# A transformer layer on one core: one more summed pair in the last gate/up block, squares written to PSUM, and another order of pairs in the second down block

## The chip, the cores and the metric

The kernel runs on one core of one Trainium2 chip. The metric is the device time of one execution in microseconds (us). A core has five engines with a queue of instructions each: TensorE (PE in the profile, with its weight loads as PEld), VectorE (DVE), ScalarE (ACT), GpSimd (POOL) and SyncE (SP), which issues most DMA transfers. Each engine executes its queue in order and waits on semaphores where an instruction needs another engine's result. All data are fp32.

## The reference, cut to what matters

The layer works on 256 positions of 2048 values. The change touches its last part, the gated feed-forward layer and the final norm:

```python
h = h + jnp.einsum('bse,ed->bsd', y, w_out[l])
u = rmsnorm(h, ln2_w[l])
ff = jax.nn.silu(jnp.einsum('bsd,df->bsf', u, w_ffn_gate[l])) * jnp.einsum('bsd,df->bsf', u, w_ffn_up[l])
h = h + jnp.einsum('bsf,fd->bsd', ff, w_ffn_down[l])
return rmsnorm(h, final_norm_w)      # h * rsqrt(mean(h * h) + eps) * final_norm_w
```

with `d` = 2048 and `f` = 5632. The projections ahead of it, a recurrence and a retention, are not touched.

## The kernel before, in words

**One product.** TensorE multiplies in a format that keeps fewer digits, so each operand is split in two: ScalarE casts it to a high part (`wh`, `ah`, `sh`, `bh`; L123) and VectorE subtracts that from the operand for the low part (`wl`, `al`, `sl`, `bl`; L124). A product of a 128x128 left with a 128x512 right is three matmuls: high times low, low times high, high times high (`three`, L683 to L685).

**Pairs.** The inner dimension is taken in pairs of 128 rows: 8 pairs for a gate/up block, 22 for a down block. With the two halves of the positions and two column blocks of 512, each pair is a 2x2 by 2x2 block product, added up in four PSUM tiles c11, c12, c21 and c22. A plain pair takes eight products (`EIGHT`). A summed pair takes seven after Winograd's form of Strassen's scheme (`SEVEN`): its operands are sums, on the left of activations (`Left`; names s, sh, sl), on the right of weights (`add`, L661, four additions on VectorE that overwrite the raw tile).

**Blocks.** Blocks 0 and 1 are the output projection, 2 to 12 the eleven gate/up blocks, 13 and 14 the two down blocks of 1024 columns each. `SUMMED` names the summed pairs of each block, `STEPS` the order of its steps: p is a plain pair and h half of one; s is the four products of a summed pair of the *next* block that all its pairs share (`share`); d is the three products that are left of a summed pair of this block (`direct`). After the last s the four shared sums are combined once (L806 to L813): p1 is a copy of c11, p = c12 - p1, q = p - c22, q goes back to c12's bank by ScalarE (L811), and c22 and c21 are corrected from q and p. The first down block has three of its summed pairs so prepared (`EARLY_DOWN`); the others of the down blocks (`SUMMED_DOWN`) are done whole, into banks p1, p5, p6 and p7, which VectorE adds to the rows `htok` once the last of them is through (`post` in `down_block`: n, part and htok rows, L923 to L934). `ORDER_DOWN` gives the order of the 22 pairs in each down block.

**Left sides.** `make_left(i)` splits the activations of pair i for the down blocks and, where the pair is summed, builds their sums. It runs when the pair's first weights are loaded.

**End of a block.** In the first down block each c is added to `htok` (L945), and `down_post` squares the row on ScalarE with a running sum (L983; the squares themselves go to an act tile `junk` that nobody reads), then multiplies the row by the norm weight `fw` (L988, deferred). The second down block ends with two plain pairs as four tails, one c after another, each cut into narrow splits.

**What sets the order.** The code is one list of steps, with weights loaded three halves ahead. The framework's scheduler then orders the instructions of each engine by a model of the chip and by priorities, which follow the order of the code; semaphores and pools do the rest. `act_tile` takes one of 60 tiles of 128x512, `raw_tile` one of 7 of 128x1024, `split_tiles` a wh and a wl out of 4, and PSUM has eight banks in two pools of four (`bank`, `aux`), chosen by the parity of the block (`room`). A tile is handed out again when the last reader of its old contents is through; whoever writes it first waits for that.

Of the kernel before, what the change touches and what calls it, by code (L numbers as in the profile page):

```python
# [28 lines left out]

SUMMED = ((), (4, 5), (2, 3), (1, 2, 3)) + ((0, 1, 2, 3),) * 8 + ((1, 2, 3),)
SUMMED_OUT, SUMMED_FFN = (4, 5), (0, 1, 2, 3)

PLAIN = ((4, 5, 6, 7, 0, 1, 2, 3),) * 2 + (tuple(range(8)),) * 11
STEPS = ("pppspppspp", "ppspdpsdpp", "pdpsdpspspp", "pspsdpsdpsdp") + ("psdhsdhsdhsdhp",) * 7 + ("psdpsdpsddp", "psdpsdpsdpp")


EARLY_DOWN = (0, 1, 2)
SUMMED_DOWN = (9, 12, 15, 17, 19), (5, 7, 9, 11, 12, 13, 15, 17, 19)  # L40
ORDER_DOWN = (3, 4, 0, 5, 6, 1, 7, 8, 2) + tuple(range(9, 22)), (0, 12, 1, 19, 2, 5, 3, 7, 4, 9, 6, 11, 8, 13, 10, 15, 14, 17, 16, 18, 20, 21)
BESIDE = (12, 19)


# [1 line left out]
def tile_hymba_layer(ctx: ExitStack, tc: tile.TileContext, A: dict, out: bass.AP):  # L46
# [22 lines left out]
    def act_tile(name, dt=F32):  # L69
        return apool.tile([P, 512], dt, tag="act", name=nm(name))  # L70
# [717 lines left out]
    class Block:  # L788
# [8 lines left out]
        def share(self, m):  # L797
            left, right, last = self.lefts[self.summed[m]], self.shared[m].parts, m == len(self.summed) - 1
            ps = self.ps
            for c, a, b in (("c11", "a11", "b11"), ("c22", "s1", "t1"), ("c21", "s3", "t3"), ("c12", "s2", "t2")):  # L800
                if m == 0:
                    ps[c] = room(self.index)(c)
                three(ps[c], left[a], right[b], m == 0, last)
            if not last:
                return

            p1, p, q = (act_tile(x) for x in ("p1", "p", "q"))
            act.copy(out=p1, in_=ps["c11"])
            v.tensor_tensor(out=p, in0=ps["c12"], in1=p1, op=ALU.subtract)
            v.tensor_tensor(out=q, in0=p, in1=ps["c22"], op=ALU.subtract)  # L810
            act.copy(out=ps["c12"], in_=q)  # L811
            v.tensor_tensor(out=ps["c22"], in0=q, in1=ps["c21"], op=ALU.subtract)
            v.tensor_tensor(out=ps["c21"], in0=ps["c21"], in1=p, op=ALU.subtract)  # L813

        def direct(self, m, quad):
            for c, a, b in DIRECT:
# [17 lines left out]
        def put(self, after):  # L834
            plain = [i for i in PLAIN[self.index] if i not in self.summed]
            for k, kind in enumerate(self.steps):
                if kind == "p":
                    i, n = plain.pop(0), len(plain)
                    quad = Quad(self.src(i), False)
                    quad.brief = n == 0  # L840
                    run = lambda i=i, quad=quad, k=k, n=n: self.plain(i, quad, k == 0, n == 0)
                elif kind == "h":
                    at = self.steps[:k].count("h") % 2
                    if not at:
                        i = plain.pop(0)
                        whole = Quad(self.src(i), False)
                    quad = HalfOf(whole, at)
                    some = slice(4 * at, 4 * at + 4)
                    run = lambda i=i, quad=whole, some=some: self.plain(i, quad, False, False, some)
                elif kind == "d":  # L850
                    m = self.steps[:k].count("d")
                    quad = Direct(self.shared[m])
                    run = lambda m=m, quad=quad: self.direct(m, quad)
                else:
                    m = self.steps[:k].count("s")
                    quad = after.shared[m]
                    run = lambda m=m: after.share(m)
                program.append(([quad], run))

    def ffn_post(j):  # L860
# [50 lines left out]
    def down_block(d, ahead):  # L911
        ps = {} if d else ahead.ps

        def tile_of(c):
            return 2 * d + int(c[2]) - 1, int(c[1]) - 1

        def into(c, a, b=None, op=ALU.add):

            h = htok[tile_of(c)]
            t = a  # L920
            if b is not None:
                t = act_tile("part")
                v.tensor_tensor(out=t, in0=a, in1=b, op=ALU.subtract)  # L923
            v.tensor_tensor(out=h, in0=h, in1=t, op=op)
            return t

        def post(c):
            if c == "p1":
                ps["a1"] = act_tile("part")
                act.copy(out=ps["a1"], in_=ps[c])  # L930
                into("c11", ps["a1"])
            elif c == "p7":
                n = act_tile("n")
                v.tensor_tensor(out=n, in0=ps["p6"], in1=ps["a1"], op=ALU.subtract)  # L934
                into("c12", n, ps["p5"])
                m = into("c21", n, ps["p7"], ALU.subtract)
                into("c22", m, ps["p5"])
            elif c[0] == "c":
                cb, t = tile_of(c)
                if d and c[:3] == "c22":  # L940
                    c0 = S * (c == "c22b")
                    down_post(cb, t, c0, S, ps[c][:, c0 : c0 + S])
                else:
                    h = htok[cb, t]
                    v.tensor_tensor(out=h, in0=ps[c], in1=h, op=ALU.add)  # L945
                    down_post(cb, t, 0, 512)

        n = FT // 2
        quads = []
        for i in ORDER_DOWN[d]:  # L950
            if d == 0 and i in EARLY_DOWN:
                quads.append(Direct(ahead.shared[EARLY_DOWN.index(i)]))
            else:
                quads.append(Quad(A["w_down"][d * n + i], i in SUMMED_DOWN[d], lambda i=i: make_left(i)))
            quads[-1].pair = i
        if d:
            quads[-1].apart = quads[-2].apart = True
        tail = [("c11", 0, 512), ("c12", 0, 512), ("c21", 0, 512)]
        def half_over():
            h = htok[3, 1][:, S:]  # L960
            act.copy(out=h, in_=ps["c22"][:, S:])
            v.tensor_tensor(out=ps["c22b"][:, S:], in0=ps["c22b"][:, S:], in1=h, op=ALU.add)

        early = {}
        if d:

            early["c22"] = lambda: v.tensor_tensor(out=ps["c22"], in0=ps["c22"], in1=htok[3, 1], op=ALU.add)
            early["c22b"] = half_over
            tail[:0] = [("c22b", S, S, slice(0, 1))]
            tail += [("c22", 0, S), ("c22b", S, S, slice(1, 4))]  # L970
        else:
            tail.append(("c22", 0, 512))

        block(NB + 2 + d, quads, dl, post, ps, tail, early=early, ordered=d == 1)

    def down_post(cb, t, c0, cw, src=None):

        h = htok[(cb, t)][:, c0 : c0 + cw]
        src = h if src is None else src
        f = fw[cb][:, c0 : c0 + cw]  # L980
        n = cb + (c0 > 0)
        j = act_tile("junk")
        act.activation(out=j[:, :cw], in_=src, func=AF.Square, accum_out=ssq[:, t, n : n + 1])  # L983
        p = pre[:, t : t + 1]
        if cb < 3:
# [278 lines left out]
```

## Time and profile before

| | before |
|---|---|
| time, median of 3 runs | 1084.82 us (1084.63 to 1085.21) |
| profiled execution | 1085.53 us |
| its span | 1083.7 us |
| granted clock of TensorE, mean | 0.996 |
| TensorE busy | 1072.3 us, 99% |
| VectorE busy | 972.0 us, 90% |
| ScalarE busy | 666.9 us, 62% |
| GpSimd busy | 56.5 us, 5% |
| DMA | 244.62 MB, 226 GB/s |

The span is the time between the first and the last instruction that the profile shows; 1.83 us of the execution lie around it. The granted clock is the share of its full speed, 2.4 GHz, that the chip gave to TensorE; 0.50 is 1.2 GHz. In a timeline a row gives the start and the duration of an instruction, or of several in a row (x3), and in brackets how long the engine had been idle before it and what ended that. Records of neighbouring matmuls overlap: the distance of their starts is what one costs.

### The profile page before, as it was taken

What the parts mean: (1) busy time and instruction counts of PE and PEld (TensorE: products, weight loads), DVE (VectorE), ACT (ScalarE), POOL (GpSimd) and SP (SyncE); (2) the same over time, 40 slices, a digit from 0 to 9 for tenths busy, and PEclk for the clock granted to TensorE, in tenths of its full rate; (3) what the DMA queues carried; (4) which work ended last, traced back from release to release, by engine and by line L of the source; (5) the groups of instructions that cost most, each with busy time, mean ns of one, the idle gap of its engine ahead of it and who ended that gap; (6) DMA issues with size and microseconds to landing.
All of it is one profiled execution on the core that took longest, in us unless ns stands there. A gap on an engine that the chain in (4) does not pass through costs nothing.

```text
span 1083.7 us, 14591 instructions
## 1 busy us (share of the span) xinstructions
PE 1072.3 (99%) x5083; PEld 897.5 (83%) x5083; DVE 972.0 (90%) x1411; ACT 666.9 (62%) x951; POOL 56.5 (5%) x73
## 2 busy tenths in 40 slices
PE   9999999999999999999999999999999999999997
PEld 7888888888888888888888888888888888878886
DVE  7789889988878889989999999999999899999886
ACT  7756744468746676656656566565656666655463
POOL 0603230000000000000000000000000010000001
PEclk9999999999999999999999999999999999999998
DMA  9964574554557587677776777776777856557662
GB/s 328 351 211 154 176 252 168 181 176 165 185 194 236 188 306 277 227 242 247 257 269 229 250 262 238 265 269 227 251 249 228 273 170 219 194 174 240 208 214 78
DMA packets 71386, 244.62 MB, mean 226 GB/s; under 512 B 8208, under 2 KB 8592, under 8 KB 71312
## 3 DMA queue, kind: packets, MB, share of 16 engines
q1 hardware_dynamic: 68400, 236.34, 64.3%
q0 software_dynamic: 1472, 4.72, 1.3%
q10 hardware_dynamic: 1440, 2.62, 0.6%
q8 instruction: 40, 0.66, 0.2%
q14 instruction: 34, 0.28, 0.1%
HBM read 239.46 MB, written 4.19 MB: 225 GB/s over the span
## 4 chain that ended last, share of the span: by engine, by line
PE 94%; POOL 1%; DMA 1%; DVE 1%; issue 1%; ACT 1%; SPq 0%; POOLq 0%; ACTq 0%
PE c L683 22%; PE c L685 22%; PE c L684 22%; PE fm L194 10%; PE fm L196 5%; PE tm L174 2%; PE tm L176 2%; PE tm L175 2%; PE p L685 1%; PE p L684 1%; PE p L683 1%; POOL sumsq L310 1%; PE ft L868 1%; DMA raw<-in_w_lx 1%; DMA raw<-in_w_v 0%
## 5 line engine op out<-in xcount | busy, mean ns | idle before, releaser
L123 ACT CAST wh<-raw 128x1024 fp32r<-128x1024 f32 (+1 forms) x500 | 464.5, 960 | 321.6 <-PE c L685 127.3
L124 DVE TENSOR_TENSOR wl<-raw,wh 128x1024 fp32r<-128x1024 f32 (+1 forms) x500 | 543.1, 1114 | 73.0 <-ACT wh L123 71.2
L684 PE MATMUL c<-wl,ah 128*128 128x512 f32 x814 | 317.7, 390 | 0.0
L685 PE MATMUL c<-wh,al 128*128 128x512 f32 x814 | 314.9, 389 | 0.0
L683 PE MATMUL c<-wh,ah 128*128 128x512 f32 x814 | 276.8, 392 | 0.0
L683 PEld LDWEIGHTS c<-wh,ah 128*128 128x128 f32 x814 | 153.4, 188 | 31.8 <-ACT wh L123 0.3
L685 PEld LDWEIGHTS c<-wh,al 128*128 128x128 f32 x814 | 152.8, 188 | 31.7 <-DVE al L124 0.3
L684 PEld LDWEIGHTS c<-wl,ah 128*128 128x128 f32 x814 | 152.9, 188 | 31.3
L194 PE MATMUL fm<-u,wh 128*128 128x512 f32 x512 | 161.3, 396 | 0.0
L196 PEld LDWEIGHTS fm<-u,wl 128*128 128x128 f32 x512 | 96.0, 188 | 22.5
L196 PE MATMUL fm<-u,wl 128*128 128x256 f32 x512 | 100.9, 278 | 0.0
L661 DVE TENSOR_TENSOR raw<-raw,raw 128x512 f32<-128x512 f32 x118 | 81.1, 688 | 2.0
L661 DVE TENSOR_TENSOR raw<-raw 128x512 f32<-128x512 f32 x118 | 80.6, 686 | 1.1
L194 PEld LDWEIGHTS fm<-u,wh 128*128 128x128 f32 x512 | 78.3, 189 | 0.3
L684 PE MATMUL c<-wl,sh 128*128 128x512 f32 x194 | 75.2, 389 | 0.0
L685 PE MATMUL c<-wh,sl 128*128 128x512 f32 x194 | 74.0, 389 | 0.0
L683 PE MATMUL c<-wh,sh 128*128 128x512 f32 x194 | 68.7, 391 | 0.3 <-ACT sh L123 0.3
L175 PE MATMUL tm<-wl,u 128*128 128x512 f32 x128 | 48.8, 394 | 0.0
L176 PE MATMUL tm<-wh,u 128*128 128x512 f32 x128 | 48.5, 390 | 0.0
L174 PE MATMUL tm<-wh,u 128*128 128x512 f32 x128 | 47.1, 398 | 0.8 <-ACT u L298 0.8
L1119 POOL DMA_DIRECT2D htok<-kept_rows x8 | 4.3, 546 | 796.4 <-DVE wl L124 704.0
L683 PEld LDWEIGHTS c<-wh,sh 128*128 128x128 f32 x194 | 36.4, 188 | 8.2 <-ACT sh L123 0.7
(247 smaller groups left out, 1076.2 us busy)
## 6 DMA issues: line engine op xcount, KB each, us to landing
raw<-in_w_gu SPq DMA_DIRECT2D x216, 512.0 KB, 5.1
raw<-in_w_down SPq DMA_DIRECT2D x91, 512.0 KB, 4.8
raw<-in_w_out SPq DMA_DIRECT2D x34, 512.0 KB, 4.3
raw<-in_w_lx SPq DMA_DIRECT2D x16, 512.0 KB, 6.9
raw<-in_w_k SPq DMA_DIRECT2D x16, 512.0 KB, 3.5
raw<-in_w_q SPq DMA_DIRECT2D x16, 512.0 KB, 3.7
raw<-in_w_rg SPq DMA_DIRECT2D x16, 512.0 KB, 3.5
raw<-in_w_lg SPq DMA_DIRECT2D x16, 512.0 KB, 3.4
```

Of the source, the lines that this page charges most:

```text
L123: act.copy(out=dst_h, in_=src)
L124: v.tensor_tensor(out=dst_l, in0=src, in1=dst_h.bitcast(F32), op=ALU.subtract)
L174: pe.matmul(ps, ah, wh, start=first, stop=False)
L175: pe.matmul(ps, ah, wl, start=False, stop=False)
L176: pe.matmul(ps, al, wh, start=False, stop=last)
L194: pe.matmul(ps, wh, hl, start=n + i == 0, stop=False)
L196: pe.matmul(ps[:, :S], wl, hl[:, :S], start=False, stop=n + i == len(order) - 1)
L310: pool.tensor_tensor(out=sumsq, in0=sumsq, in1=sq, op=ALU.add)
L661: v.tensor_tensor(out=dst, in0=a, in1=b, op=ALU.add)
L683: pe.matmul(p, ah, bh, start=first, stop=False, skip_group_check=onto)
L684: pe.matmul(p, ah, bl, start=False, stop=False, skip_group_check=onto)
L685: pe.matmul(p, al, bh, start=False, stop=last, skip_group_check=onto)
```

## The change

Block 12, the last gate/up block, gets four summed pairs like the others, and the steps of blocks 11 and 12 follow: block 11 is now "psdhsdhsdhsdhp" and block 12 "psdpsdpsddp". The six instructions that combine the shared sums are given a higher priority (offset 300) in all blocks. `ASIDE` lets block 12 make the lefts of down pairs 1 to 4 ahead of its steps 0, 2, 4 and 6. In the second down block the first two pairs are plain ones, and the pairs behind them are ordered anew; near the end, summed pair 17 stands ahead of 16, 18, 20 and 21 before, and behind 16 now. In the first down block the squares of the norm are written over the PSUM bank of the c that has just been added, in place of an act tile; in the second they stay as they are. Line numbers move by one to four: L123 is now L124, L811 is L813, L983 is L987, L988 is L992.

```diff
--- before.py
+++ after.py
@@ -29,16 +29,17 @@
 
 
 
-SUMMED = ((), (4, 5), (2, 3), (1, 2, 3)) + ((0, 1, 2, 3),) * 8 + ((1, 2, 3),)
+SUMMED = ((), (4, 5), (2, 3), (1, 2, 3)) + ((0, 1, 2, 3),) * 9
 SUMMED_OUT, SUMMED_FFN = (4, 5), (0, 1, 2, 3)
 
 PLAIN = ((4, 5, 6, 7, 0, 1, 2, 3),) * 2 + (tuple(range(8)),) * 11
-STEPS = ("pppspppspp", "ppspdpsdpp", "pdpsdpspspp", "pspsdpsdpsdp") + ("psdhsdhsdhsdhp",) * 7 + ("psdpsdpsddp", "psdpsdpsdpp")
+STEPS = ("pppspppspp", "ppspdpsdpp", "pdpsdpspspp", "pspsdpsdpsdp") + ("psdhsdhsdhsdhp",) * 8 + ("psdpsdpsddp",)
 
 
 EARLY_DOWN = (0, 1, 2)
+ASIDE = {(12, 0): 1, (12, 2): 2, (12, 4): 3, (12, 6): 4}
 SUMMED_DOWN = (9, 12, 15, 17, 19), (5, 7, 9, 11, 12, 13, 15, 17, 19)
-ORDER_DOWN = (3, 4, 0, 5, 6, 1, 7, 8, 2) + tuple(range(9, 22)), (0, 12, 1, 19, 2, 5, 3, 7, 4, 9, 6, 11, 8, 13, 10, 15, 14, 17, 16, 18, 20, 21)
+ORDER_DOWN = (3, 4, 0, 5, 6, 1, 7, 8, 2) + tuple(range(9, 22)), (0, 1, 12, 2, 19, 3, 5, 4, 7, 6, 9, 8, 11, 10, 13, 14, 15, 16, 17, 18, 20, 21)
 BESIDE = (12, 19)
 
 
@@ -805,12 +806,13 @@
                 return
 
             p1, p, q = (act_tile(x) for x in ("p1", "p", "q"))
-            act.copy(out=p1, in_=ps["c11"])
-            v.tensor_tensor(out=p, in0=ps["c12"], in1=p1, op=ALU.subtract)
-            v.tensor_tensor(out=q, in0=p, in1=ps["c22"], op=ALU.subtract)
-            act.copy(out=ps["c12"], in_=q)
-            v.tensor_tensor(out=ps["c22"], in0=q, in1=ps["c21"], op=ALU.subtract)
-            v.tensor_tensor(out=ps["c21"], in0=ps["c21"], in1=p, op=ALU.subtract)
+            with tc.high_priority(offset=300):
+                act.copy(out=p1, in_=ps["c11"])
+                v.tensor_tensor(out=p, in0=ps["c12"], in1=p1, op=ALU.subtract)
+                v.tensor_tensor(out=q, in0=p, in1=ps["c22"], op=ALU.subtract)
+                act.copy(out=ps["c12"], in_=q)
+                v.tensor_tensor(out=ps["c22"], in0=q, in1=ps["c21"], op=ALU.subtract)
+                v.tensor_tensor(out=ps["c21"], in0=ps["c21"], in1=p, op=ALU.subtract)
 
         def direct(self, m, quad):
             for c, a, b in DIRECT:
@@ -855,6 +857,8 @@
                     m = self.steps[:k].count("s")
                     quad = after.shared[m]
                     run = lambda m=m: after.share(m)
+                if (self.index, k) in ASIDE:
+                    program.append(([], lambda i=ASIDE[self.index, k]: make_left(i)))
                 program.append(([quad], run))
 
     def ffn_post(j):
@@ -943,7 +947,7 @@
                 else:
                     h = htok[cb, t]
                     v.tensor_tensor(out=h, in0=ps[c], in1=h, op=ALU.add)
-                    down_post(cb, t, 0, 512)
+                    down_post(cb, t, 0, 512, gone=None if d else ps[c])
 
         n = FT // 2
         quads = []
@@ -973,13 +977,13 @@
 
         block(NB + 2 + d, quads, dl, post, ps, tail, early=early, ordered=d == 1)
 
-    def down_post(cb, t, c0, cw, src=None):
+    def down_post(cb, t, c0, cw, src=None, gone=None):
 
         h = htok[(cb, t)][:, c0 : c0 + cw]
         src = h if src is None else src
         f = fw[cb][:, c0 : c0 + cw]
         n = cb + (c0 > 0)
-        j = act_tile("junk")
+        j = act_tile("junk") if gone is None else gone
         act.activation(out=j[:, :cw], in_=src, func=AF.Square, accum_out=ssq[:, t, n : n + 1])
         p = pre[:, t : t + 1]
         if cb < 3:
```

Up to some 775 us of the run all engines have the same rows in the same order. Over the whole run TensorE has 3 matmuls fewer, VectorE 7 rows more (four raw additions and three splits), ScalarE 3 more and SP one load more. Three places are shown. The names in the rows are tiles, with a running number that differs between the two kernels.

ScalarE at the start of the second down block, before: casts of weights (`wh`, `bh`) and the four squares of the first down block (L983), in the order of the queue.

```order
L123 CAST wh_1951_9147<-raw_1950_9145 128x1024
L123 CAST wh_1954_9153<-raw_1953_9151 128x1024
L123 CAST wh_1957_9159<-raw_1956_9157 128x1024
L123 CAST bh_1960_9165<-raw_1959_9163 128x512
L123 CAST wh_1967_9231<-raw_1966_9229 128x1024
L983 ACTIVATE junk_1962_9182,ssq_120<-htok_1826_8628 128x512
L123 CAST wh_1969_9239<-raw_1959_9163 128x1024
L983 ACTIVATE junk_1963_9197,ssq_120<-htok_1828_8632 128x512
L983 ACTIVATE junk_1964_9212,ssq_120<-htok_1827_8630 128x512
L983 ACTIVATE junk_1965_9227,ssq_120<-htok_1829_8634 128x512
L123 CAST bh_1984_9289<-raw_1983_9287 128x512
L123 CAST wh_1971_9243<-raw_1966_9229 128x1024
```

And now (the squares are L987):

```order
L124 CAST wh_1962_9172<-raw_1961_9170 128x1024
L124 CAST wh_1965_9178<-raw_1964_9176 128x1024
L124 CAST bh_1971_9246<-raw_1970_9244 128x512
L124 CAST wh_1968_9240<-raw_1967_9238 128x1024
L987 ACTIVATE c11_1678_7960,ssq_120<-htok_1831_8641 128x512
L987 ACTIVATE c12_1681_7972,ssq_120<-htok_1833_8645 128x512
L987 ACTIVATE c21_1680_7968,ssq_120<-htok_1832_8643 128x512
L124 CAST wh_1978_9280<-raw_1977_9278 128x1024
L124 CAST bh_1991_9334<-raw_1990_9332 128x512
L987 ACTIVATE c22_1679_7964,ssq_120<-htok_1834_8647 128x512
L124 CAST wh_1980_9288<-raw_1970_9244 128x1024
L124 CAST wh_1982_9292<-raw_1977_9278 128x1024
```

Each square now writes to the bank of the c that it belongs to; three stand together ahead of the casts of the first summed pair, and the fourth behind two of these.

VectorE at the end of block 12, before: p, q and the two corrections (L809 to L813), among splits of weights (`wl`, wide) and of lefts (`al`, narrow).

```order
L124 TENSOR_TENSOR wl_1726_8162<-raw_1722_8155,wh_1725_8161 128x1024
L809 TENSOR_TENSOR p_1714_8126<-c12_1668_7925,p1_1713_8125 128x512
L810 TENSOR_TENSOR q_1715_8127<-p_1714_8126,c22_1666_7917 128x512
L124 TENSOR_TENSOR wl_1734_8202<-raw_1730_8195,wh_1733_8201 128x1024
L812 TENSOR_TENSOR c22_1666_7917<-q_1715_8127,c21_1667_7921 128x512
L813 TENSOR_TENSOR c21_1667_7921<-c21_1667_7921,p_1714_8126 128x512
L124 TENSOR_TENSOR wl_1739_8238<-raw_1737_8235,wh_1738_8237 128x1024
L124 TENSOR_TENSOR al_1724_8158<-ff_1013_4924,ah_1723_8157 128x512
L124 TENSOR_TENSOR wl_1742_8244<-raw_1740_8241,wh_1741_8243 128x1024
L124 TENSOR_TENSOR al_1732_8198<-ff_1092_5290,ah_1731_8197 128x512
```

And now (p is L811, q L812, the corrections L814 and L815; L883 is the gating of block 12's own outcome):

```order
L125 TENSOR_TENSOR t4l_1715_8110<-raw_1711_8097,t4h_1714_8109 128x512
L811 TENSOR_TENSOR p_1726_8168<-c12_1681_7972,p1_1725_8167 128x512
L125 TENSOR_TENSOR wl_1739_8215<-raw_1737_8212,wh_1738_8214 128x1024
L125 TENSOR_TENSOR wl_1747_8257<-raw_1745_8254,wh_1746_8256 128x1024
L812 TENSOR_TENSOR q_1727_8169<-p_1726_8168,c22_1679_7964 128x512
L125 TENSOR_TENSOR wl_1744_8251<-raw_1742_8248,wh_1743_8250 128x1024
L883 SCALAR_TENSOR_TENSOR gated_1740_8224<-c12_1590_7573,r2_tok_110,gated_1740_8224 128x512
L883 SCALAR_TENSOR_TENSOR gated_1741_8232<-c22_1588_7565,r2_tok_110,gated_1741_8232 128x512
L125 TENSOR_TENSOR wl_1759_8314<-raw_1752_8298,wh_1758_8313 128x1024
L814 TENSOR_TENSOR c22_1679_7964<-q_1727_8169,c21_1680_7968 128x512
L815 TENSOR_TENSOR c21_1680_7968<-c21_1680_7968,p_1726_8168 128x512
```

Two wide splits stand between p and q now, and the corrections of c22 and c21 behind the gating.

VectorE near the end of the second down block, before: the last summed pair's additions to the rows (n is L934, part L923, htok L924) and the narrow splits (`bl`) of the last two pairs. The difference n, two parts and two wide splits stand ahead of these rows.

```order
L924 TENSOR_TENSOR htok_2040_9569<-htok_2040_9569,part_2124_9984 128x512
L924 TENSOR_TENSOR htok_2039_9567<-htok_2039_9567,part_2125_9987 128x512
L923 TENSOR_TENSOR part_2126_9990<-part_2125_9987,p5_1987_9303 128x512
L124 TENSOR_TENSOR bl_2132_10005<-raw_2130_10002,bh_2131_10004 128x512
L124 TENSOR_TENSOR bl_2134_10009<-raw_2130_10002,bh_2133_10008 128x512
L124 TENSOR_TENSOR bl_2137_10039<-raw_2135_10036,bh_2136_10038 128x512
L124 TENSOR_TENSOR bl_2139_10043<-raw_2135_10036,bh_2138_10042 128x512
L924 TENSOR_TENSOR htok_2041_9571<-htok_2041_9571,part_2126_9990 128x512
L124 TENSOR_TENSOR bl_2142_10049<-raw_2140_10046,bh_2141_10048 128x512
L124 TENSOR_TENSOR bl_2144_10053<-raw_2140_10046,bh_2143_10052 128x512
L124 TENSOR_TENSOR bl_2147_10084<-raw_2145_10081,bh_2146_10083 128x512
L124 TENSOR_TENSOR bl_2149_10088<-raw_2145_10081,bh_2148_10087 128x512
```

And now (n is L938, part L927, htok L928, L971 an addition of htok to c22's bank); n and one part stand right ahead:

```order
L927 TENSOR_TENSOR part_2134_10036<-n_2132_10031,p7_1996_9356 128x512
L928 TENSOR_TENSOR htok_2041_9581<-htok_2041_9581,part_2133_10033 128x512
L928 TENSOR_TENSOR htok_2040_9579<-htok_2040_9579,part_2134_10036 128x512
L927 TENSOR_TENSOR part_2135_10039<-part_2134_10036,p5_1994_9348 128x512
L125 TENSOR_TENSOR bl_2138_10048<-raw_2136_10045,bh_2137_10047 128x512
L125 TENSOR_TENSOR bl_2140_10052<-raw_2136_10045,bh_2139_10051 128x512
L928 TENSOR_TENSOR htok_2042_9583<-htok_2042_9583,part_2135_10039 128x512
L125 TENSOR_TENSOR bl_2143_10058<-raw_2141_10055,bh_2142_10057 128x512
L125 TENSOR_TENSOR bl_2145_10062<-raw_2141_10055,bh_2144_10061 128x512
L125 TENSOR_TENSOR bl_2148_10093<-raw_2146_10090,bh_2147_10092 128x512
L971 TENSOR_TENSOR c22_1975_9258<-c22_1975_9258,htok_2042_9583 128x512
L125 TENSOR_TENSOR bl_2150_10097<-raw_2146_10090,bh_2149_10096 128x512
```

No wide split stands between n and the last narrow split any more; the additions to the rows and the narrow splits are interleaved, and the last split stands behind the addition to c22, which came after all of them before.

## Rows read from the trace of the kernel before

**Rows 1.** Page, busy time (us), share of the span and instructions of each engine.

```profile
PE 1072.3 (99%) x5083; PEld 897.5 (83%) x5083; DVE 972.0 (90%) x1411; ACT 666.9 (62%) x951; POOL 56.5 (5%) x73
```

**Rows 2.** Timeline of TensorE, second down block: start, duration, instruction, idle before it.

```profile
1061.05 0.39 PE L685 MATMUL c<-wh,al 128*128 128x512 f32 x1
...
1064.45 0.39 PE L685 MATMUL c<-wh,al 128*128 128x512 f32 x1
...
1067.32 0.39 PE L684 MATMUL c<-bl,ah 128*128 128x512 f32 x1
1067.55 0.39 PE L685 MATMUL c<-bh,al 128*128 128x512 f32 x1
```

**Rows 3.** Stretches: busy us of PE, PEld, DVE, ACT, POOL; granted clock; DMA share; GB/s.

```profile
969.00:972.00 3.00, 3.00 (x8) 2.30 (x7) 3.00 (x4) 2.53 (x3) 0.00 (x0) 0.50 0.26 90
775.00:820.00 45.00, 45.00 (x205) 37.30 (x204) 40.99 (x55) 26.83 (x36) 0.00 (x0) 1.00 0.74 246
820.00:861.00 41.00, 41.00 (x186) 33.71 (x185) 37.24 (x51) 27.30 (x35) 0.00 (x0) 1.00 0.78 257
963.00:973.00 10.00, 8.66 (x29) 6.16 (x28) 8.94 (x12) 7.91 (x14) 0.00 (x0) 0.83 0.29 97
8.00:13.00 5.00, 4.17 (x19) 3.08 (x18) 3.91 (x14) 4.33 (x9) 0.00 (x0) 1.00 0.93 336
```

**Rows 4.** Timeline of TensorE, start of the second down block.

```profile
965.69 0.39 PE L683 MATMUL p<-wh,sh 128*128 128x512 f32 x1
966.86 0.50 PE L684 MATMUL p<-wl,sh 128*128 128x512 f32 x1 [0.79 <-DVE wl L124]
...
968.65 1.00 PE L683 MATMUL p<-wh,sh 128*128 128x512 f32 x2 [0.45 <-ACT wh L123]
969.44 0.63 PE L684 MATMUL p<-wl,sh 128*128 128x512 f32 x1
...
972.62 0.39 PE L684 MATMUL p<-wl,sh 128*128 128x512 f32 x1
```

**Rows 5.** Timeline of ScalarE, start of the second down block.

```profile
956.41 1.05 ACT L123 CAST wh<-raw 128x1024 fp32r<-128x1024 f32 x1 [0.59 <-PE c L685]
963.62 0.63 ACT L983 ACTIVATE junk<-htok 128x512 f32<-128x512 f32 x1 [6.16 <-PE c L684]
...
964.25 1.04 ACT L123 CAST wh<-raw 128x1024 fp32r<-128x1024 f32 x1
...
967.55 2.94 ACT L123 CAST wh<-raw 128x1024 fp32r<-128x1024 f32 x3
```

**Rows 6.** Timeline of VectorE, start of the second down block.

```profile
953.16 0.68 DVE L923 TENSOR_TENSOR part<-n,p 128x512 f32<-128x512 f32 x1
953.87 0.69 DVE L924 TENSOR_TENSOR htok<-htok,part 128x512 f32<-128x512 f32 x1
...
964.38 0.69 DVE L988 TENSOR_TENSOR htok<-htok,fw 128x512 f32<-128x512 f32 x1 [1.06 <-ACT junk L983]
...
965.59 1.22 DVE L124 TENSOR_TENSOR wl<-raw,wh 128x1024 fp32r<-128x1024 f32 x1
```

**Rows 7.** Timeline of VectorE, end of the second down block.

```profile
1050.61 3.50 DVE L124 TENSOR_TENSOR wl<-raw,wh 128x1024 fp32r<-128x1024 f32 x3 [1.19 <-ACT wh L123]
...
1059.89 2.49 DVE L124 TENSOR_TENSOR bl<-raw,bh 128x512 fp32r<-128x512 f32 x4
...
1062.90 2.49 DVE L124 TENSOR_TENSOR bl<-raw,bh 128x512 fp32r<-128x512 f32 x4
...
1067.97 0.69 DVE L945 TENSOR_TENSOR htok<-c,htok 128x512 f32<-128x512 f32 x1 [1.10 <-PE c L685]
```

**Rows 8.** Line 811: duration in ns, smallest, median, largest.

```profile
L811 ACT COPY c<-q x13: 572/583/600, 332.8 to 849.5; 128x512 f32<-128x512 f32 x13
```

**Rows 9.** Timeline of VectorE, end of block 12.

```profile
842.54 2.58 DVE L124 TENSOR_TENSOR wl<-raw,wh 128x1024 fp32r<-128x1024 f32 x2 [0.32 <-ACT wh L123]
846.16 1.23 DVE L124 TENSOR_TENSOR wl<-raw,wh 128x1024 fp32r<-128x1024 f32 x1 [1.04 <-ACT wh L123]
```

## The prediction

> **What bounds the kernel now.** I read the page's busy times first. TensorE is busy in 99% of the span and VectorE in 90% [rows 1], so a change gains time by taking matmuls away, or by closing the few places where TensorE waits. VectorE is so near that any work added to it must be followed. Next the timeline of TensorE, for its step: from 1061.05 to 1064.45 us there are 15 matmuls of 128x512, 0.2267 us each [rows 2]. Its record of 0.39 us is longer because neighbours overlap; I count steps.
>
> Then the stretches. From 775 us on the granted clock is 1.00 everywhere but at the start of the second down block, where it is 0.83 over 963 to 973 us and 0.50, the 1.2 GHz level, over 969 to 972 us [rows 3]. That place has two losses [rows 4]. From 965.69 to 968.65 us only four matmuls go out, which need 0.91 us of the 2.96: 2.05 us of waits. From 968.65 to 972.62 us ten go out, 2.27 us of 3.97: 1.70 us for the half clock that follows. Together 3.75 us.
>
> The cause stands on ScalarE [rows 5]. The first square (L983) waited 6.16 us for TensorE: not for its input, but for a tile out of the pool into which it writes a result that nobody reads; a matmul of the second down block had to release it. The casts behind it in ScalarE's queue then ran late: at 964.25 us, and three wide ones from 967.55 us on. VectorE waited 1.06 us with its product by the norm weight (L988) for that square, and the low part that TensorE missed at 966.86 us ran only at 965.59 [rows 6].
>
> **The change part by part.** The sums are made against the profiled execution, 1085.53 us (span 1083.7 and 1.83 around it), which is 0.71 above the median of the runs, 1084.82. All rows up to some 775 us stand in the same order as before, so I follow only what comes later.
>
> *Fourth summed pair in block 12.* A summed pair takes seven products where a plain one takes eight: three matmuls fewer, 3 x 0.2267 = **-0.68 us**. VectorE gets four raw additions (4 x 0.60) and, splits of three narrow and two wide rows for the plain pair's two wide ones (4.1 less 2.3): 4.2 us more. One more load of 512 KB goes through SP's queue; the DMA engines are 0.74 to 0.78 busy there [rows 3], and I price it at nothing as long as a load lands in time.
>
> *Squares into PSUM.* The square now writes over the bank from which its sum was just taken, so it waits for that VectorE addition alone, and no act tile is asked for. The 6.16 us of ScalarE waiting go, and with them the 2.05 and the 1.70 us: **-3.75 us**. The second edit works for the same end: with pairs 0 and 1 plain, 48 matmuls (10.9 us) lie between the end of the first down block and the first product of a summed pair. What could keep the loss is a square that holds its bank too long: p1 of pair 12 waits for the square of c11. That bank closes 56 matmuls ahead, 12.7 us; addition, a wide cast in ScalarE's queue and the square take 0.42 + 0.69 + 1.05 + 0.63 = 2.8 us [rows 2, 5, 7]. So 9.9 us remain. A copy from SBUF into PSUM took 0.583 us (0.572 to 0.600) [rows 8] and the square into SBUF 0.63 [rows 5], so the four squares cost ScalarE between 0.2 us less and nothing less; it has idle time. The Trainium skill's page "ScalarE: Activation LUTs" (section "Step-by-step: what each stage is for") says that ScalarE writes PSUM sooner than SBUF, but that this helps only where TensorE doesn't need most of PSUM. Here TensorE uses all eight banks, so by the caveat the waits would stay (rival four); the rows speak against it.
>
> *Second down block, first summed pair.* What is late next is p6 of pair 12, whose cast needs the last of the raw additions. From the closing of c11 VectorE runs 21 rows up to that addition, four wide (1.14 each, a third and a half of the 3.50 us group [rows 7]) and 17 narrow (0.602: 2.49 us for four less the last one's 0.685, over three): 4 x 1.137 + 16 x 0.602 + 0.685 = 14.87 us. With 0.42 until VectorE sees a closed bank (1067.55 to 1067.97 [rows 2, 7]), 0.05 for each hand-over (966.81 to 966.86 [rows 4, 6]) and the cast of 1.05 that is 16.44. TensorE has 71 matmuls up to there, 16.10. So **+0.4 us** (0.34 and a little idle between). Bounds: nothing, if VectorE is let go sooner, and 2, the waits seen at this place before.
>
> *Combination with priority, block 12 to first down block.* The order shows q (L812 now) behind two wide splits, where before it stood right behind p. The copy of q into c12's bank must be there for the first plain product on it, 20 matmuls (4.53 us) after c12 closes. VectorE and ScalarE need 0.42 + 0.60 + 2 x 1.137 + 0.685 + 0.05 + 0.583 + 0.05 = 4.66. That is 0.13 if VectorE reaches p on time, 0.73 if it comes one narrow row late, 1.27 with a wide one. VectorE idled 0.32 and 1.04 us just ahead of p before [rows 9], and now has more to do. I take **+0.5 us**; bounds 0 and 1.27. Lefts 1 to 4 made beside block 12 are the same instructions earlier, two of them out of the down block: 1.2 us more there for VectorE.
>
> *Tail.* The order 17, 16 in place of 16, 17 puts the last summed pair one plain pair nearer the end. Behind the end of its p6 VectorE now runs 14 rows without a pause up to the last narrow split: the difference n, which the next row needs (0.71, as at 953.16 and 953.87 [rows 6]), 12 x 0.602, and the split itself 0.685. With 0.42 and 0.05 that is 9.09 us. TensorE has 34 matmuls before it needs that split, 7.71 us. **+1.4 us**. Before, the same split ended at 1065.39 (2.49 us from 1062.90 [rows 7]) for a matmul at 1067.32 [rows 2], 1.93 us of spare time; the pair moved eats that. Bounds: nothing, if the queue is not in that order in time, and 3.0, if the two wide splits ahead of n are themselves just in time.
>
> Sum: -0.68 - 3.75 + 0.4 + 0.5 + 1.4 = -2.13 us. That is 1083.40 for a run like the profiled one and **1082.7 us** against the median. What the runs of this kernel can tell from no change is about 0.2%, 2.17 us, so this lies on the border: 1082.65.
>
> **The rivals.** *One: no new wait.* VectorE runs some microseconds ahead, as its idle 1.04 us shows [rows 9], and the three waits close. Against it: the tail's sum starts at a matmul, and no lead helps it. -4.43 us: 1080.4.
>
> *Two: the half clock comes back.* The new waits cost what the old one did: after 2.05 us of waits the clock stood at 0.50 for 1.70 us of loss [rows 3, 4]. For it: the tail's 1.4 us in one piece. Against it: from 8 to 13 us TensorE was idle for 0.83 of 5 us with the clock at 1.00 [rows 3]. One such loss gives 1084.4, two 1086.1. By the Trainium skill, "TensorE: Matmul & The Clock Gate" (section "Part 1: The HAM clock gate"), the clock follows how busy TensorE has been lately; by that rule the tail falls to half speed and the time is this rival's 1084.4. The trace has a place for each answer.
>
> *Three, the other side: VectorE becomes the bound* in blocks 11 and 12. From 775 to 861 us it is busy 40.99 + 37.24 = 78.2 of 86 us [rows 3], and 4.2 + 1.2 us come in: 83.6 of 85.3. If its idle 7.8 us were forced (waits for casts and for tiles, not spare time), the 5.4 us would fall on TensorE, and one half clock with them: -2.13 + 5.4 + 1.7 = +5.0, 1089.8 us. It is slower than before from the point at which over 4.3 of these 7.1 us arrive. Against it: the matmuls need fewer operands in these blocks, not more.
>
> *Four: the loss only moves.* VectorE's queue rather than ScalarE's holds the start of the second down block, or a bank is held; then only -0.68 remains: 1084.1.
>
> **How the numbers follow.** The forecast 0.40, with its own range 1081.5 to 1084.0 (each of the three waits from nearly none to half as much again); no new wait 0.26; half clock 0.18; VectorE the bound 0.11; moved loss 0.05. Faster by over 0.2%: half of the first and all of the second, and a little of the third, 0.48. Slower by over 0.2% (above 1086.99): the VectorE case and a trace of the half clock, 0.12. The rest, 0.40, within 0.2%. The range reaches from just under rival one, 1080.2, to two half clocks, 1086.3; what it leaves out is rival three and the far end of one.
>
> **What would show it.** In the changed kernel's profile the squares (L987) should wait for a VectorE addition, no longer for TensorE; 963 to 973 us should have the clock at 1.00. TensorE's waits should stand at three places: for the ACT copy of q (L813) near 852 us, for an ACT cast ahead of p6 near 971 us, and for VectorE's split `bl` some 15 us before the end. TensorE's count should fall by three. I am wrong if the tail shows no wait for that split (then the time is nearer to 1080.4), if the granted clock falls anywhere behind a new wait, or if TensorE waits for VectorE all through blocks 11 and 12.

## The result, and the profile after

| | time, median (range), us | ratio to before, 95% interval |
|---|---|---|
| before, beside it | 1084.92 (1084.63 to 1085.23), 5 runs | |
| changed kernel | 1089.92 (1086.60 to 1091.48), 5 runs | 1.0041 [1.0030, 1.0052] |
| changed kernel, second series | 1087.57 (1086.00 to 1089.25), 5 runs | 1.0032 [1.0019, 1.0044] |

Each series is set against runs of the kernel before taken beside it; for the second these are 21 with a median of 1084.44 us. The change makes the kernel slower, by 0.3 to 0.4%, and its runs lie further apart: 4.9 and 3.3 us between the lowest and the highest of five, where the kernel before has 0.6 in five runs and 2.0 in a later series of 33. The profiled execution took 1091.48 us (span 1089.7). Busy times on the page after [rows 1]:

```profile
PE 1076.2 (99%) x5080; PEld 896.9 (82%) x5080; DVE 975.9 (90%) x1418; ACT 667.2 (61%) x954; POOL 56.4 (5%) x73
```

Stretches of the changed kernel [rows 3], columns as there:

```profile
775.00:820.00 45.00, 45.00 (x204) 37.32 (x203) 42.63 (x57) 27.23 (x36) 0.00 (x0) 1.00 0.76 263
820.00:861.00 41.00, 40.52 (x187) 33.09 (x186) 38.02 (x55) 27.17 (x39) 0.00 (x0) 1.00 0.72 245
963.00:973.00 10.00, 10.00 (x46) 8.29 (x45) 10.00 (x15) 3.81 (x7) 0.00 (x0) 1.00 0.30 100
1000.00:1060.00 60.00, 59.41 (x257) 47.22 (x256) 48.93 (x57) 31.36 (x36) 0.00 (x0) 1.00 0.59 201
1072.00:1075.00 3.00, 3.00 (x8) 2.33 (x8) 1.03 (x4) 1.39 (x3) 0.60 (x1) 0.50 0.00 0
```

The start of the second down block now runs at full clock, 10.00 us busy of 10. In place of the one stall there are many waits. TensorE's waits after 10 us, by releaser (total us, times, longest):

```profile
PE c L685 <- DVE bl L125: 1.7, 2, 1.4
PE c L684 <- ACT wh L124: 0.9, 4, 0.2
PE p L684 <- ACT wh L124: 0.6, 1, 0.6
PE c L684 <- ACT c L813: 0.5, 1, 0.5
```

And the places, from its timeline (start, duration, instruction, idle before it) [rows 4]:

```profile
853.59 0.39 PE L684 MATMUL c<-wh,ah 128*128 128x512 f32 x1
854.45 0.50 PE L684 MATMUL c<-wh,ah 128*128 128x512 f32 x1 [0.48 <-ACT c L813]
...
974.47 0.39 PE L686 MATMUL p<-wh,sl 128*128 128x512 f32 x1
975.42 0.73 PE L684 MATMUL p<-wh,sh 128*128 128x512 f32 x2 [0.56 <-ACT wh L124]
...
1028.46 0.39 PE L684 MATMUL c<-wh,ah 128*128 128x512 f32 x1
1029.08 0.96 PE L684 MATMUL c<-wh,ah 128*128 128x512 f32 x3 [0.23 <-ACT wh L124]
...
1069.92 0.40 PE L684 MATMUL c<-bh,ah 128*128 128x512 f32 x1
1071.74 0.66 PE L685 MATMUL c<-bl,ah 128*128 128x512 f32 x1 [1.43 <-DVE bl L125]
1072.20 0.63 PE L686 MATMUL c<-bh,al 128*128 128x512 f32 x1
...
1075.50 0.40 PE L685 MATMUL c<-bl,ah 128*128 128x512 f32 x1
```

They are, in order: the copy of q at the end of block 12 (two steps of 0.86 and 0.34 us for 0.45, a loss of 0.75); the cast ahead of the first p6 (0.95 and 0.34: 0.83); a cast in one of the later couples of a summed and a plain pair, of which there are six with 0.3 to 0.6 us and 2.52 together; and the last split `bl` in the tail, 1.82 for one step, after which the steps are 0.43 us until 1075.50: the clock of 0.50 in the last stretch above. The tail costs 2.34 in waits and 1.70 in clock. Near 937 us, in the first down block, 1.06 us more are lost to casts; in ScalarE's queue they stand behind a narrow cast `bh` that had waited 2.65 us for its load (first row; the second is TensorE's):

```profile
931.35 0.62 ACT L124 CAST bh<-raw 128x512 fp32r<-128x512 f32 x1 [2.65 <-DMA raw<-in_w_down]
...
938.73 0.96 PE L684 MATMUL c<-wh,ah 128*128 128x512 f32 x3 [0.21 <-ACT wh L124]
```

A part of the 5.95 us between the two profiled executions is no effect of the change. The same transposes, before any row is moved, start at 776.14 us before and at 777.21 now:

```profile
776.14 0.82 PE L868 MATMUL ft<-ident,gated 128*128 128x128 f32 x6
```

```profile
777.21 0.82 PE L872 MATMUL ft<-ident,gated 128*128 128x128 f32 x6
```

From there to the end of the last matmul the changed kernel takes 304.85 us, before 299.75: 5.10 more. Losses by steps: -0.68 (three matmuls), -3.75 (start of the second down block), +0.63 (block 12), +1.06, +0.83, +2.52, +4.04 (tail) = +4.65; 0.45 is in steps too small to tell. In the second series' profile, 1086.00 us, these transposes start at 775.36 and the same sum is +1.1 (1.4 measured up to the last matmul): the waits at block 12, 937 us, p6 and the tail are the same within 0.02, but the couples lose 0.66 and the clock stays up. So a run's time hangs on the loads in the couples, on the clock behind the tail's wait, and on its first 775 us.

```profile
775.36 0.82 PE L872 MATMUL ft<-ident,gated 128*128 128x128 f32 x6
```

### The profile page after: what moved, and what is told of

Its sections match the earlier page's. It is cut to its first block, busy times and chain, and to the rows that moved or that the text cites. A ratio compares the mean times of both kernels' runs of the same rounds, so it can differ in the third digit from the quotient of the medians.

```text
span 1089.7 us, 14602 instructions
## 1 busy us (share of the span) xinstructions
PE 1076.2 (99%) x5080; PEld 896.9 (82%) x5080; DVE 975.9 (90%) x1418; ACT 667.2 (61%) x954; POOL 56.4 (5%) x73
## 4 chain that ended last, share of the span: by engine, by line
PE 80%; DVE 8%; DMA 4%; issue 3%; ACT 2%; POOL 1%; SPq 0%; ACTq 0%; POOLq 0%; DVEq 0%
PE c L684 18%; PE c L685 18%; PE c L686 18%; PE fm L195 10%; PE fm L197 5%; DMA raw<-in_w_down 4%; DVE wl L125 3%; PE tm L175 3%; PE tm L176 3%; PE tm L177 3%; DVE raw L662 2%; ACT wh L124 2%; POOL sumsq L311 1%; DVE bl L125 1%; PE ft L872 1%
## 5 line engine op out<-in xcount | busy, mean ns | idle before, releaser
L124 ACT CAST wh<-raw 128x1024 fp32r<-128x1024 f32 (+1 forms) x502 | 464.8, 958 | 325.8 <-PE c L686 115.4
L684 PEld LDWEIGHTS c<-wh,ah 128*128 128x128 f32 x808 | 151.1, 188 | 35.7 <-ACT wh L124 4.3
```

Of the source, the lines that this page charges most:

```text
L124: act.copy(out=dst_h, in_=src)
L684: pe.matmul(p, ah, bh, start=first, stop=False, skip_group_check=onto)
```

## The experiments

With every edit the scheduler orders the queues anew, so each comes with other places for the rows near it. What TensorE loses at a place is counted in steps, as above.

**Squares alone.** To the kernel before (shortened; in the first down block the bank of the c is handed over as `gone`):

```diff
-        j = act_tile("junk")
+        j = act_tile("junk") if gone is None else gone
```

> The kernel before with the squares of the first down block written to PSUM, nothing else. Theory (VectorE's queue holds the start of the second down block, not the act tile): ScalarE's wait of 6.16 us goes, and TensorE's waits at 966 to 972 us stay with 2 to 5 us, half clock among them; 1084 to 1087. My prediction's step (the act tile holds it): the 3.75 us go, 1081.

Measured: 1089.38 us, ratio 1.0047 [1.0034, 1.0060]. ScalarE's 6.16 us wait is gone, as expected; the squares run at 957.40 us and wait for VectorE alone. The stall is not gone: the casts of the first summed pair are late all the same, the narrow one at 963.25 us for a tile that TensorE releases, the wide ones for VectorE's additions; TensorE loses 4.27 us there and 2.87 more at 988 to 995 us. ScalarE's timeline of this run:

```profile
957.40 0.60 ACT L983 ACTIVATE c<-htok 128x512 f32<-128x512 f32 x1 [0.31 <-DVE htok L945]
...
963.25 0.62 ACT L123 CAST bh<-raw 128x512 fp32r<-128x512 f32 x1 [1.59 <-PE c L684]
...
968.14 3.89 ACT L123 CAST wh<-raw 128x1024 fp32r<-128x1024 f32 x4 [2.49 <-DVE raw L661]
```

VectorE in the 16 us ahead (busy DVE the third figure):

```profile
953.00:969.00 16.00, 14.12 (x62) 11.03 (x60) 15.47 (x23) 8.07 (x14) 0.00 (x0) 1.00 0.36 125
```

My reading of the wait was wrong: the act tile was the last to be waited for, and with that wait gone the casts wait for VectorE's additions instead. Expected 1084 to 1087; it was worse. Where the 2.87 us at 988 to 995 us come from stays open.

**The old order in the changed kernel.** `ORDER_DOWN[1]` put back, all else as changed.

> The changed kernel with the old order of the second down block alone put back (fourth summed pair, ASIDE, squares to PSUM stay). Theory (the new order costs, the other parts do not): the wait for the last narrow split and the half clock behind it (3.7 us) go, and so do the waits of each couple; the start of the second down block depends on who held it. If it was the act tile of the squares, it is free: 1081 to 1083. If VectorE's queue held it, it stays with 3 to 4 us: 1084.5 to 1086.5. Rival three (VectorE bound by the fourth pair in blocks 11 and 12): waits of some us stay between 775 and 861 us and the time stays near 1089.

Measured: 1089.31 us, 1.0042 [1.0030, 1.0055]. The tail is clean; the start of the second down block loses 6.33 us, half clock in it, with VectorE busy 15.79 of 16 us ahead:

```profile
953.00:969.00 16.00, 13.83 (x61) 10.92 (x59) 15.79 (x24) 6.88 (x13) 0.00 (x0) 0.99 0.29 112
```

So squares and fourth pair do not take the stall away, it is longer with them; the theory's second branch had the place right and the size too small.

**The new order alone,** in the kernel before.

> The kernel before with the new order of the second down block alone (no fourth pair, squares still into act tiles). Theory: the order alone does both, it takes the 3.75 us of the block's start away and brings the waits of each couple (2 to 3.5) and the tail with its half clock (3 to 3.7): 1086 to 1089. If the act tile of the squares held the start, the 6 us wait of ScalarE stays as well and the time goes over 1089. If the fourth pair makes the loss (rival three), the time is 1081 to 1083.

Measured: 1086.33 us, 1.0019 [1.0011, 1.0028], at the low end. In its profile the start loses 0.17 us in place of 3.75, with the squares still in act tiles; the couples lose 2.17 and the tail 2.34. The order takes the stall away and brings both waits.

How busy VectorE is does not tell a stall from none. Over the same 16 us it is busy 15.82 here and 15.79 in the changed kernel (second row), as much as in the two runs above that stall, but TensorE (first figure behind the length) is busy for all 16:

```profile
953.00:969.00 16.00, 16.00 (x73) 13.24 (x72) 15.82 (x24) 8.48 (x15) 0.00 (x0) 1.00 0.56 207
953.00:969.00 16.00, 16.00 (x72) 13.26 (x71) 15.79 (x22) 8.78 (x15) 0.00 (x0) 1.00 0.67 235
```

This fits the prediction's second reason: with two plain pairs first, TensorE has work in hand while VectorE gets the summed pair ready.

The tail's wait in this run:

```profile
1068.27 0.50 PE L684 MATMUL c<-bl,ah 128*128 128x512 f32 x1 [1.44 <-DVE bl L124]
```

**The fourth pair alone,** with its steps and early lefts, in the kernel before. (The run is the changed kernel with the old order and the act tiles put back; the higher priority stays in it.)

> The kernel before with the fourth summed pair, its steps and the early lefts alone. Theory: 0.68 us of matmuls less, 0.7 us of waits more at the end of block 12, up to 1 us near 937 us, the stall at 966 us as before: within 1.5 us of the kernel before, 1084 to 1086. Rival three (VectorE bound by the fourth pair): 1088 or more.

Measured: 1085.74 us, 1.0010 [1.0001, 1.0019]. The wait for q (0.75) is the whole of what is new before 930 us; rival three falls. The stall costs 2.64 us here, without half clock, 937 us 0.22 and the couples 1.0. No run has the changed kernel with nothing but the squares put back; the order (1.0019) and the fourth pair (1.0010) together come near to the change's 1.0032 and 1.0041.

**The tail.** In the changed kernel:

```diff
-(..., 13, 14, 15, 16, 17, 18, 20, 21)
+(..., 13, 15, 14, 17, 16, 18, 20, 21)
```

> The changed kernel with summed pair 17 ahead of plain pair 16 again (and 15 ahead of 14), so that four plain pairs end the block as before. Theory: the wait for the last narrow split (1.8 us) and the half clock behind it (1.7 us) go, 3 to 4 us less than the changed kernel; the waits in each couple stay. If the tail was merely the end of the late loads: less than 1 us.

Measured: 1088.26 us, 1.0033 [1.0021, 1.0046]. The tail's wait is gone (0 us after 1062), but summed pairs 13 and 15 side by side wait 2.14 us in one step at 1041.79 and bring the half clock there: 5.5 us in the couples. The 3 to 4 us that I expected did not come: the place moved, and little was gained.

```profile
1043.93 0.50 PE L684 MATMUL p<-wh,sh 128*128 128x512 f32 x1 [1.74 <-ACT wh L124]
```

**Lead.** In the changed kernel, ahead of the first product of the second down block:

```diff
+                    if ordered and m == 0:
+                        for _ in range(5):
+                            three(p, lefts[quads[q].pair][a], right, True, True, True)
```

> The changed kernel with 15 matmuls more (5 x the first product of the second down block, each thrown away), 3.4 us of TensorE at full speed. Lead theory: in the second down block the weights come at one couple of pairs (a summed and a plain one) in 10.6 us, while TensorE needs 45 x 0.2267 = 10.2; what TensorE loses at the start of the block is lead for the casts, so the waits of 0.8 us at 974 us and of 0.3 to 0.6 us in each of six couples (3.5 us together) go, and the time is within 1 us of the changed kernel. Rival (these waits have nothing to do with the lead): all of the 3.4 us is added.

Measured: 1088.48 us (1087.74 to 1089.04), 1.0035 [1.0023, 1.0048]: 3.4 us of work for 0.35 us more than the median of the changed kernel's ten runs, 1088.13; by its ratio it lies between the two series (1.0032 and 1.0041). In its profile the wait at 974 us is gone (0.83), but the couples still lose 1.22, where I expected none. In them the changed kernel itself lost 2.52 in one profile and 0.66 in the other, so the lead takes the first wait away, and whether it helps the couples stays open.

**Who holds the couples.** ScalarE in the changed kernel (first the square that waits for nobody, then casts):

```profile
961.61 0.59 ACT L987 ACTIVATE c<-htok 128x512 f32<-128x512 f32 x1
...
1001.25 0.62 ACT L124 CAST bh<-raw 128x512 fp32r<-128x512 f32 x1 [3.77 <-DMA raw<-in_w_down]
1001.77 1.05 ACT L124 CAST wh<-raw 128x1024 fp32r<-128x1024 f32 x1
1005.64 3.89 ACT L124 CAST wh<-raw 128x1024 fp32r<-128x1024 f32 x4 [2.82 <-DVE raw L662]
...
1054.17 1.14 ACT L124 CAST bh<-raw 128x512 fp32r<-128x512 f32 x2 [2.12 <-DMA raw<-in_w_down]
```

The narrow cast bh of the next summed pair stands in ScalarE's queue ahead of the wide casts of the present one, and waits 3.77 us for its load. From 1001.25 to 1054.17 us there are five couples: 10.58 us each. TensorE needs 45 x 0.2267 = 10.20. Before, it was the same (three couples, 10.61):

```profile
1004.39 0.62 ACT L123 CAST bh<-raw 128x512 fp32r<-128x512 f32 x1 [1.43 <-DMA raw<-in_w_down]
...
1036.23 0.62 ACT L123 CAST bh<-raw 128x512 fp32r<-128x512 f32 x1 [2.22 <-DMA raw<-in_w_down]
```

There it showed only as a shrinking lead: TensorE's p6 (its `p<-wh,sh`) came 2.68 us after the end of its cast in the couple at 1002 us, then 2.47, 2.08, 1.76 and 1.23. The first and the last of these (of a row x2 or x3 the first cast counts, 1.05 us long):

```profile
998.38 2.00 ACT L123 CAST wh<-raw 128x1024 fp32r<-128x1024 f32 x2 [1.49 <-DVE raw L661]
1002.11 0.39 PE L683 MATMUL p<-wh,sh 128*128 128x512 f32 x1
...
1040.63 2.96 ACT L123 CAST wh<-raw 128x1024 fp32r<-128x1024 f32 x3 [2.83 <-DVE raw L661]
1042.91 0.39 PE L683 MATMUL p<-wh,sh 128*128 128x512 f32 x1
```

The stall at 966 us may have built that lead, but no run shows it: three others stall there too and still lose in the couples, 0.7 us with the old order in the changed kernel, 1.0 with the fourth pair alone, 3.5 with the squares alone. The test is to let bh wait for half a load, in the changed kernel and in the kernel before:

```diff
+            for o in (0, 512) if self.sums and half == 0 else (None,):
...
+                    nc.sync.dma_start(out=r[:, o : o + 512], in_=self.src[:, o : o + 512])
```

> The changed kernel with the first half of every whole summed pair of the down blocks loaded in two transfers of 256 KB, so that the narrow cast bh, which needs 512 of the 1024 columns, waits for the first alone. Theory (in each couple bh stands in ScalarE's queue ahead of the casts that TensorE needs next, and waits for its load): the bh waits for DMA (15 to 18 us in all) shrink, the waits of the couples (0.7 to 2.5 us) and near 937 us (1 us) go, those at 853, 974 and 1069 us stay: 1 to 3 us less than the changed kernel, 1085.5 to 1087. If VectorE's load sets the couples' pace, nothing changes: 1087.5 to 1090.

Measured: 1084.62 us, 1.0004 [0.9995, 1.0012], below the range that I expected; the changed kernel stood at 1.0032 and 1.0041. The couples and 937 us lose 0.00, and bh comes every 10.14 us:

```profile
997.86 0.62 ACT L124 CAST bh<-raw 128x512 fp32r<-128x512 f32 x1 [1.67 <-DMA raw<-in_w_down]
...
1048.55 1.14 ACT L124 CAST bh<-raw 128x512 fp32r<-128x512 f32 x2 [1.80 <-DMA raw<-in_w_down]
```

Its waits for the DMA shrink little, from 15.6 us in the second profile to 14.2; what counts is that they end earlier. From 1000 to 1060 us the first half lands 3.3 us after its issue (3.8 once), where the whole load took 3.7 to 4.1. From 1015 us on all engines have the same rows in the same order as in the changed kernel, so in the last couples the load alone makes the difference; from 904 to 1015 us rows moved as well, and at 937 us load and order are not told apart.

> The kernel before with the split loads alone. Theory: nothing to gain, since the stall at the start of the second down block (2 to 3.75 us) comes from VectorE's queue and gives the couples their lead: within 1 us of the kernel before.

Measured: 1085.43 us, 1.0006 [0.9998, 1.0015]: nothing by itself.

**Better orders.** First, in the kernel before:

> The kernel before with another order of the second down block alone: two plain pairs first, as in the change, then summed and plain pairs in turn, with summed pairs 9 and 11 next to each other in the middle, so that the block ends as before (17, 16, 18, 20, 21). Theory: the stall at 966 us goes (3.75 us), the tail has no wait for the last split, and the waits of late couples are fewer, since the plain pair that is saved stands among them: 1081 to 1083, faster than both. If the lead is all that counts, the couples take back 2 to 3 us: 1083.5 to 1085.

Measured: 1084.99 us, 1.0007 [0.9998, 1.0015]: start 0.17 and tail 0 as expected, but the neighbours 9 and 11 wait 1.68 us in one step; 2.27 us in the couples, as the second branch has it.

> The same order and eight summed pairs without the split loads. Theory: +0.68 for the product, no stall at the start and no wait in the tail, waits of 1 to 2.5 us in the couples: 1083 to 1084.5.

Measured: 1084.09 us, 0.9997 [0.9988, 1.0006]; couples 2.29, at the top of what was expected, and 0.57 at the first p6.

> The kernel before with split loads as in the run beside it, and the second down block as 0, 1, 12, 2, 19, 3, 5, 4, 7, 6, 9, 8, 11, 10, 13, 14, 15, 17, 16, 18, 20, 21 with eight summed pairs (15 is plain): two plain pairs first, no two summed ones side by side, the end as before. One product more: +0.68. Theory: all four waits are gone (start 3.75, couples, tail), 1081 to 1082.5, faster than both kernels. If the couples' waits come from VectorE: 1083.5 to 1085.

Measured: 1082.78 us (1081.83 to 1083.61), 0.9984 [0.9975, 0.9993], faster than both kernels, by 1.8 us against the one before, and 0.3 above the range that I expected. All waits of TensorE over 0.2 us after 10 us are gone but the second of these, which lies at 372 us, ahead of the change, and stands in the kernel before too (the first was over at 9.76 us):

```profile
PE tm L174 <- ACT u L298: 0.7, 1, 0.7
PE c L687 <- ACT sh L123: 0.3, 1, 0.3
```

**The changed kernel again.**

> The changed kernel once more, for its spread and a second profile. Theory: what differs from run to run is how late the loads land in the second down block and whether the clock falls behind the wait of the tail; 1086 to 1091, and in the profile the waits at 853, 974 and 1069 us again, each within 0.3 us of the first profile, those of the couples less so.

Measured: in the table above, with the waits as expected. The half clock did not come back, though the wait in the tail was the same. TensorE's timeline there, and the stretch behind it with the clock ahead of the last two figures:

```profile
1067.84 0.50 PE L685 MATMUL c<-bl,ah 128*128 128x512 f32 x1 [1.43 <-DVE bl L125]
```

```profile
1069.00:1072.00 3.00, 3.00 (x15) 2.48 (x14) 1.26 (x4) 2.21 (x4) 1.28 (x1) 1.00 0.00 0
```

## Why the prediction was wrong, by its own steps

The forecast was 1082.7 in 1080.2 to 1086.3; the measured 1089.92 lies above it, on the side to which I gave 0.12.

*Three matmuls fewer.* Right: 5083 to 5080 on the page.

*"One more load ... I price it at nothing as long as a load lands in time."* This is the step that failed: late loads at no price, and with it -3.75 as a full gain and waits "at three places" alone. It is not the one added load. The loads of summed pairs in the down blocks as a whole came late for the narrow casts. They cost 2.52 us in the couples of one profile and 0.66 of the other, and 1.06 and 1.04 near 937 us, in the first down block, ahead of any stall; of the kernels whose loads are not split, only those with the fourth pair lose anything there (0.11 to 1.06). Splitting the loads gave some 3 us back. I looked at the durations of TensorE's stall and not at the stretch behind it: in the trace of before the casts came every 10.61 us for 10.20 of matmuls, which could have been read there.

Between my sum, -2.13, and the +4.65 of the first profile lie 6.78 us: 3.58 in the couples and near 937 us, 1.70 of the clock, 0.94 of the tail, 0.43 of p6 and 0.13 of block 12. In the second profile it is 3.2 us, with 1.70 in the couples and near 937 us and none of the clock.

*Squares into PSUM, -3.75 us.* The stall went, but the order took it away, not the squares (0.17 us left with the order alone, 4.27 with the squares alone). So the size came out by the second of my two reasons, the plain pairs ahead; the first was wrong, and by itself the edit costs 0.47%. The last wait to end was taken for the cause; with it gone, the casts waited for VectorE's additions. That the squares run shorter into PSUM held, by little: 0.58 to 0.59 us in the changed kernel against 0.61 to 0.63 before. The Trainium skill's page "ScalarE: Activation LUTs" (section "Step-by-step: what each stage is for") says that ScalarE is faster into PSUM than into SBUF, and the traces agree. Its caveat on a TensorE that needs most of PSUM does not show in the changed kernel: no wait of TensorE there names a square.

*First p6, +0.4.* Right place, and with 0.83 us twice the size, inside its bounds.

*Copy of q, +0.5.* Right place, 0.75: one narrow row late. The priority around it did nothing: built without it, all engines have the same rows in the same order. So the place of q came from the fourth pair, its steps and its early lefts (the run with these alone has the same wait).

*Tail, +1.4.* The mechanism was right and the size off: 2.34 us. I let the 14 rows start 0.42 us after the end of p6, but n ran at 1063.07, behind wide splits, three where my upper bound had named two:

```profile
1059.65 3.50 DVE L125 TENSOR_TENSOR wl<-raw,wh 128x1024 fp32r<-128x1024 f32 x3 [0.60 <-ACT wh L124]
1063.07 0.68 DVE L938 TENSOR_TENSOR n<-p,part 128x512 f32<-128x512 f32 x1
...
1071.00 0.68 DVE L125 TENSOR_TENSOR bl<-raw,bh 128x512 fp32r<-128x512 f32 x1
```

*Rival two* came true in one of the two profiles: 1.70 us. *Rival three* gave nearly the measured time, 1089.8, by a mechanism that is not there: VectorE is busy 42.63 + 38.02 = 80.7 of 86 us in blocks 11 and 12, and the fourth pair alone costs 0.1%. (Its "over 4.3 of these 7.1 us" is the point of 0.2% slower; slower at all it is from 2.13 on.)

## What to carry to other kernels

Before counting the removal of a stall as a gain, compare the period of what feeds the bound engine behind the stall with the engine's own, in the trace of before (10.61 against 10.20 us a couple, here over some six couples). A wait has one releaser in the profile, but another engine can be just as late: take the named cause away alone before building on it (the squares alone: 0.47% slower). And where a narrow instruction waits for a large transfer ahead of others in an in-order queue, try letting it go with the part that it needs: here that took the waits of the couples away, but gave nothing in the kernel before, where TensorE did not wait in them.

## What the runs showed of the hardware

The clock fell to 0.50 for 3.4 us after the tail's wait of 1.43 us in one run of the changed kernel, and stayed at 1.00 after the same wait of 1.43 in another and in two experiments (2.34 us of loss each). In the changed kernel from 1000 to 1040 us a load of 512 KB landed 3.1 to 3.3 us after its issue when it was alone; of three that were issued 1.1 us apart, the first took 3.8 to 4.1, the second 4.2 to 5.3 and the third 5.0 to 5.4.
